# Half of an output sum moved from VectorE to accumulating transfers, and four more modulation products given to TensorE

## Chip, cores and metric

The kernel runs on one NeuronCore of one Trainium2 chip. The metric is device time in microseconds of one execution; the time before is the median of three runs. A separate execution was profiled, and its rows are those below.

## What is computed

Two layers of a diffusion backbone work on 512 latent tokens and 256 context tokens, each with 1024 features, in fp32. A layer is a SwiGLU feed-forward half (FFN), a mixing block, and a second FFN. Each FFN does

```python
y = swiglu(modulate(rms_norm(h, g), m[:, 3 * i], m[:, 3 * i + 1]), w1, w3, w2)
return h + 0.5 * m[:, 3 * i + 2, None, :] * y
```

where `m = silu(c) @ w + b` holds nine modulation vectors of 1024 for each layer, one set for the tokens and one for the context. The hidden width is 2816, in 22 blocks of 128.

## The kernel before

The residual `h` stands transposed in SBUF: eight tiles `h[d]` of 128 features by 768 columns, the context in columns 0 to 255 and the latent tokens in 256 to 767. Every fp32 product is made of three passes over split operands (`mm3`, lines 402 to 407): high times high, high times low, low times high. Weights are loaded raw by SP's queue and split by ScalarE (`L412`, or `L415` with a factor) and VectorE (`L413`, `L416`).

An FFN (`ffn7`) takes the 22 hidden blocks in 11 pairs. A middle pair (`pair`) computes its two blocks for both weight matrices with seven products in place of eight (Strassen's scheme), each of 24 matmuls 384 columns wide, in two PSUM tiles Y and X. The order in the program is: B11 into Y; then `middle()`, which is the whole w2 part of the pair before; then `y0`, a copy of Y that ScalarE makes (`snapshot`, line 742); B21 into X; E added into Y; t3 into X; t1, t4, B22. E may not begin before `y0` is taken, because it adds into the bank that `y0` copies; t3 may not begin before `gated` has read X and `y0`. Further copies (`y1` after E, `w0` after t3) follow in the same way.

`middle(j)` goes over the two halves of the eight tiles of `h`, in each half over the context columns and then the latent columns, in each over four tiles d: `down` makes 6 matmuls into one of four PSUM banks and VectorE adds the gated result into `h[d]` (line 760). When both halves are done, the pair's `g` tiles are given back, and `modulate(j)` puts `mods[j]` groups of modulation rows in the queue, at a much lower priority (`later(3000)`): each group loads four `ada` tiles (`mod_group`, line 500; on SP in the first FFN, on GpSimd's queue in the second) and VectorE makes six row-by-column products from them (line 492). In layer 0 the first FFN has such groups with middles 1 to 8 (`mods=(0,) + (2,) * 8`), the second with middles 2 to 7.

The order in which an engine takes its instructions is made when the kernel is built: the program order gives priorities, and a scheduler with a model of the engines places the ready instruction of highest priority. On the chip each engine then follows its own list.

SBUF tiles of 768 columns come from 44 slots. `m3` takes the slot that has been free for longest, `free` puts one at the end of the list:

```python
i = self.free_slots.popleft()
t = self.mp.tile([128, n], dt, tag=f"m{i}", name=self.name(base), bufs=1)
self.slot_of[t.tensor.name] = i
```

A new tile may be written only when every reader of the tile that had the slot before is done, transfers included. In a middle pair 35 slots are held: 16 by the normed input n, 12 by combinations of it, 3 by the broadcast condition, 4 by the g of the pair before. That leaves nine.

The start (`Start`, layer 0 only) makes the first 2048 modulation values. For each of eight feature tiles k, `item(k)` loads 1 MB of modulation weights, and `mods(k)` makes shift and scale: for k in `ON_PE` on TensorE (32 passes of 128x2, line 224, and two small VectorE instructions, line 228), for the others with VectorE (line 492) for the tokens and with GpSimd and ScalarE (lines 484 and 486) for the context. Then `norm(k)` makes the normed tile (lines 285 to 289), and 12 matmuls of 512 and 9 or more of 256 columns use it. Before, `ON_PE` is `(0,)`.

Of the kernel before, what the change touches and what calls it, by code (L numbers as in the profile page):

```python
# [11 lines left out]
AF = mybir.ActivationFunctionType  # L12
ALU = mybir.AluOpType
# [23 lines left out]
C_COLS = (0, CTX)  # L37
X_COLS = (CTX, T)
# [132 lines left out]
def mod_order(i):  # L171

    return (i // 2 + 8 * (i % 2)) if i < 16 else i


class Start:

    LAG = 1
    ON_PE = (0,)
    AHEAD = 2  # L180
    LOADS = 3

# [33 lines left out]
    def mods(self, k):  # L216

        b, nc = self.b, self.b.nc
        it = self.items.pop(k)
        if k in self.ON_PE:  # L220
            ps = b.ps("B", 3)
# [8 lines left out]
        else:  # L230
            for s in range(2):
                with b.later(60 * s):
                    for q in (1, 0):
                        b.mod_tile(0, q * 8 + k, s, (it[q], it[2][:, q * 256:q * 256 + 256]), pool=s == 1)
                    self.derive(k, s, 1)
        if k in self.ON_PE:
            self.derive(k, 0, 2)
# [84 lines left out]
class Builder:  # L322
# [335 lines left out]
        self.split_psum(w[:, 0], w[:, 1], r, scale)  # L658
        return w

    def ffn7(self, l, i, n, t, gate, nxt, streams=(X_COLS, C_COLS), split=None, late=None, mods=(), begin=None):

# [8 lines left out]
        nc = self.nc  # L673
# [75 lines left out]
            self.last_silu = nc.scalar.activation(s[:, cols], zv[:, 0], AF.Silu, scale=sign)  # L749
            nc.vector.scalar_tensor_tensor(out=s[:, cols], in0=zv[:, 1], scalar=sign, in1=s[:, cols], op0=ALU.mult, op1=ALU.mult)  # L750

        def down(fs, ws, d, cols):
            c0, c1 = cols
            s = 1 if c0 < CTX else 0
            ps = self.psB()
            for x in (1, 0):
                o = x * 512 + d % 4 * 128
                self.mm3(ps[:, 0:c1 - c0], [ws(d // 4)[:, p, o:o + 128] for p in range(2)],
                         (g[fs[x]][0][:, c0:c1], g[fs[x]][1][:, c0:c1]), x == 1, x == 0)
            nc.vector.scalar_tensor_tensor(out=self.h[d][:, c0:c1], in0=ps[:, 0:c1 - c0], scalar=gate()[:, d, s:s + 1],  # L760
                                           in1=self.h[d][:, c0:c1], op0=ALU.mult, op1=ALU.add)

# [86 lines left out]
        def second(j):  # L849

            ws = {}
            return lambda half: ws[half] if half in ws else ws.setdefault(half, self.unit(w2[j, half]))
# [53 lines left out]
        def middle(j):  # L906
            def go():
                ws, fs = second(j), (2 * j, 2 * j + 1)
                for half in range(2):
                    for cols in streams[::-1]:  # L910
                        for d in range(half * 4, half * 4 + 4):
                            down(fs, ws, d, cols)
                self.free([g.pop(f) for f in fs])
                modulate(j)
            return go

        def modulate(j):
            with self.later(3000):
                for _ in range(min(mods[j] if j < len(mods) else 0, len(self.mod_queue))):
                    self.mod_queue.pop(0)()  # L920
# [5 lines left out]
        fs = (NF - 2, NF - 1)  # L926
        if x_only:
            pair(np_ - 1, middle(np_ - 2))
        else:
            held = {}  # L930

            def go():
                held["ws"], held["fs"] = second(np_ - 2), (NF - 4, NF - 3)
                for d in range(8):
                    down(held["fs"], held["ws"], d, X_COLS)

            pair(np_ - 1, go)
            for d in range(8):
                down(held["fs"], held["ws"], d, C_COLS)
            self.free([g.pop(f) for f in held["fs"]])  # L940
            modulate(np_ - 2)
        ws = second(np_ - 1)
# [707 lines left out]
    def gate(self, l, mod, ns, f):  # L1650
        box = []

        def get():
            if not box:
                box.append(self.derive_gate(l, mod, ns, f))
            return box[0]
        return get

    def build(self, stop=None):
        nc = self.nc  # L1660
        self.setup()
        n = self.new_n()
        begin = Start(self, n)
        for g in range(5, 24):
            self.mod_queue.append(lambda g=g: self.mod_group(0, g, 16))
        for l in range(DEPTH):
            last = l == DEPTH - 1
            ns = 1 if last else 2
            nxt = Next(self, l, 3, SM_GMIX, 2, n)
            if l:  # L1670
                tabs = []
                self.ffn7(l, 0, n, t, self.gate(l, 2, 2, 0.5), nxt, late=lambda: tabs.extend(self.late_tables(l)), mods=(0,) * 2 + (2,) * 6)
            else:
                tabs = []
                self.ffn7(l, 0, n, {}, self.gate(l, 2, 2, 0.5), nxt, late=lambda: tabs.extend(self.late_tables(l)),
                          mods=(0,) + (2,) * 8, begin=begin)
            assert not self.mod_queue
            if l == 0:
                self.setup_mixing()
            if stop == (l, 0):  # L1680
                break

            nxt = Next(self, l, 6, SM_GF2, ns, keep=X_HALVES if last else T_HALVES)
            self.mixing(l, n, tabs, self.gate(l, 5, ns, 1.0), last, nxt)
            n, before = nxt.n, nxt
            if stop == (l, 1):
                break

            if not last:
                self.load_small(l + 1)  # L1690
                self.silu_c(wide=True)
                for g in range(24):
                    self.mod_queue.append(lambda g=g: self.mod_group(1, g))
                nxt = Next(self, l + 1, 0, SM_GF1, 2, n, keep=T_HALVES)
                self.ffn7(l, 1, n, before.t, self.gate(l, 8, 2, 0.5), nxt, mods=(0,) * 2 + (2,) * 6)
                t = nxt.t
            else:
                self.ffn7(l, 1, n, before.t, self.gate(l, 8, 1, 0.5), Done(self), streams=(X_COLS,), split=X_HALVES)
            if stop == (l, 2):
                break  # L1700
        if stop is not None:
            for k in range(8):
                nc.sync.dma_start(self.a["out"][k], self.h[k])
# [40 lines left out]
def pack(inp):  # L1744
# [12 lines left out]
    tra = np.concatenate([tra[..., 0:768].reshape(8, 128, 1536), tra[..., 768:].reshape(8, 128, 512)], -1)  # L1757
    o["ada0"] = np.stack([(nat if k in Start.ON_PE else tra)[k] for k in range(8)])
    wa = a["w_ada"].transpose(0, 2, 1).reshape(L, 72, 128, D)[:, [mod_order(i) for i in range(72)]]
# [65 lines left out]
```

## Time and profile before

| what | value |
|---|---|
| median of 3 runs | 2718.38 us (2717.03 to 2721.74) |
| profiled execution | 2715.82 us, span of the core 2714.0 us |
| mean granted TensorE clock | 0.982 of full speed |
| busy: TensorE / VectorE / ScalarE / GpSimd | 96% / 78% / 43% / 14% |

The busy shares are averages over the span. TensorE is granted one of two clock levels, 1.2 and 2.4 GHz, and a share of 1.00 means the higher one throughout. "Idle before" is the time that an engine did nothing ahead of an instruction, with the instruction or transfer that ended it.

### The profile page before, as it was taken

The numbers are of one execution on the slowest core, as the hardware profiler recorded it, in microseconds if no ns is written. First come the engines' busy times: TensorE is split into PE (matmuls) and PEld (weight loads), VectorE is DVE, ScalarE is ACT, GpSimd is POOL, SyncE is SP. The second block draws the span as 40 slices with busy tenths as digits, with TensorE's granted clock in tenths as the row PEclk, the third lists the DMA queues.
The fourth block names the chain that finished last, engine by engine and source line by source line (L and its number), as shares of the span: only waits on it lengthen the run. The fifth ranks groups of instructions, "written<-read, shape, count | busy, mean of one in ns | idle before, by whom it ended". The sixth has DMA issues, their size and how long they took to land.

```text
span 2714.0 us, 40079 instructions
## 1 busy us (share of the span) xinstructions
PE 2599.7 (96%) x15572; PEld 2351.3 (87%) x15572; DVE 2121.0 (78%) x3664; ACT 1168.5 (43%) x2042; POOL 383.8 (14%) x530
## 2 busy tenths in 40 slices
PE   6899999999989999999999999999999899999999
PEld 4788989898867778999899889999998777889998
DVE  8998989975685647899996778888766775588887
ACT  6532333244665654233333633323234765554443
POOL 4300000010352212010000211100001452110000
PEclk8999999999999999999999999999999999999999
DMA  6634444321200014344332334443221200143322
GB/s 242 164 115 123 131 122 135 117 84 53 74 24 17 20 47 101 120 137 133 119 99 71 80 92 140 137 149 121 82 86 53 80 15 24 42 114 108 95 94 93
DMA packets 81889, 261.51 MB, mean 96 GB/s; under 512 B 10018, under 2 KB 19874, under 8 KB 81700
## 3 DMA queue, kind: packets, MB, share of 16 engines
q1 hardware_dynamic: 64804, 209.67, 24.0%
q0 software_dynamic: 16896, 49.29, 7.4%
q8 instruction: 122, 2.00, 0.3%
q14 instruction: 67, 0.55, 0.1%
HBM read 245.29 MB, written 2.10 MB: 91 GB/s over the span
## 4 chain that ended last, share of the span: by engine, by line
PE 80%; DVE 10%; issue 3%; ACT 3%; DMA 3%; POOL 1%; SPq 0%; DVEq 0%; POOLq 0%; ACTq 0%
PE S L405 14%; PE S L407 14%; PE S L406 14%; PE B L405 10%; PE B L406 10%; PE B L407 10%; PE B L1334 3%; DVE cst L492 2%; PE B L1485 2%; DVE w L413 1%; DVE h L760 1%; DMA nf<-nf 1%; DMA ada<-in_w_ada 1%; PE B L1453 1%; DVE nf L285 1%
## 5 line engine op out<-in xcount | busy, mean ns | idle before, releaser
L412 ACT CAST w<-raw 128x1024 fp32r<-128x1024 f32 (+1 forms) x387 | 403.8, 1045 | 630.6 <-PE B L407 304.1
L413 DVE TENSOR_TENSOR w<-raw,w 128x1024 fp32r<-128x1024 f32 (+1 forms) x387 | 474.9, 1228 | 95.4 <-ACT w L412 94.3
L405 PE MATMUL S<-nhi,w 128*128 128x384 f32 (+2 forms) x1520 | 493.6, 331 | 38.0 <-ACT y L742 22.5
L406 PE MATMUL S<-nlo,w 128*128 128x384 f32 (+2 forms) x1520 | 499.9, 330 | 3.1 <-DVE nlo L615 2.0
L407 PE MATMUL S<-nhi,w 128*128 128x384 f32 (+2 forms) x1520 | 499.7, 330 | 1.0 <-DVE w L413 0.9
L760 DVE SCALAR_TENSOR_TENSOR h<-B,g,h 128x512 f32<-128x512 f32 (+1 forms) x616 | 377.3, 633 | 126.4 <-PE B L407 123.3
L406 PE MATMUL B<-glo,w 128*128 128x512 f32 (+1 forms) x1232 | 421.4, 346 | 0.0
L407 PE MATMUL B<-ghi,w 128*128 128x512 f32 (+1 forms) x1232 | 420.6, 345 | 0.0
L405 PE MATMUL B<-ghi,w 128*128 128x512 f32 (+1 forms) x1232 | 408.1, 347 | 7.6 <-DVE h L760 6.5
L405 PEld LDWEIGHTS S<-nhi,w 128*128 128x128 f32 x1520 | 288.9, 192 | 49.9 <-ACT y L742 24.9
L406 PEld LDWEIGHTS S<-nlo,w 128*128 128x128 f32 x1520 | 291.9, 192 | 11.7 <-DVE nlo L615 3.9
L406 PE MATMUL S<-clo,w 128*128 128x384 f32 (+1 forms) x936 | 301.4, 322 | 0.0
L405 PE MATMUL S<-chi,w 128*128 128x384 f32 (+1 forms) x936 | 301.3, 322 | 0.0
L407 PEld LDWEIGHTS S<-nhi,w 128*128 128x128 f32 x1520 | 291.4, 192 | 10.3 <-DVE w L413 4.4
L407 PE MATMUL S<-chi,w 128*128 128x384 f32 (+1 forms) x936 | 299.3, 323 | 0.0
L407 PEld LDWEIGHTS B<-ghi,w 128*128 128x128 f32 x1232 | 232.4, 189 | 30.1
L405 PEld LDWEIGHTS B<-ghi,w 128*128 128x128 f32 x1232 | 227.8, 188 | 35.4 <-DVE h L760 8.7
L406 PEld LDWEIGHTS B<-glo,w 128*128 128x128 f32 x1232 | 232.2, 188 | 25.3 <-issue 0.7
L492 DVE CUSTOM_DVE_ANT_0 cst<-ada,bc,mpart 128x768 f32<-128x768 f32 x238 | 246.3, 1035 | 3.2 <-DMA ada<-in_w_ada 1.6
L405 PEld LDWEIGHTS S<-chi,w 128*128 128x128 f32 x936 | 176.1, 188 | 3.7
L406 PEld LDWEIGHTS S<-clo,w 128*128 128x128 f32 x936 | 176.0, 188 | 3.2
L407 PEld LDWEIGHTS S<-chi,w 128*128 128x128 f32 x936 | 175.1, 188 | 2.2
(261 smaller groups left out, 4344.9 us busy)
## 6 DMA issues: line engine op xcount, KB each, us to landing
raw<-in_w13s SPq DMA_DIRECT2D x176, 512.0 KB, 3.4
raw<-in_w2s SPq DMA_DIRECT2D x88, 512.0 KB, 3.5
ada<-in_w_ada POOLq DMA_DIRECT2D x96, 384.0 KB, 3.8
ada<-in_w_ada SPq DMA_DIRECT2D x75, 384.0 KB, 3.7
nf<-nf POOLq DMA_DIRECT2D x48, 192.0 KB, 4.0
raw<-in_w_out SPq DMA_DIRECT2D x16, 512.0 KB, 3.8
ada<-in_ada SPq DMA_DIRECT2D x16, 384.0 KB, 5.9
raw<-in_w_in_t SPq DMA_DIRECT2D x10, 512.0 KB, 3.4
```

Of the source, the lines that this page charges most:

```text
L285: nc.vector.scalar_tensor_tensor(out=t, in0=b.h[k][:, c0:c1], scalar=a, in1=self.R[cols], op0=ALU.mult, op1=ALU.mult)
L405: mm(out, lhs[0], rhs[0], start=start, stop=False, skip_group_check=more)
L406: mm(out, lhs[0], rhs[1], start=False, stop=False, skip_group_check=more)
L407: mm(out, lhs[1], rhs[0], start=False, stop=stop, skip_group_check=more)
L412: nc.scalar.copy(hi, src)
L413: nc.vector.tensor_sub(lo, src, hi.bitcast(F32))
L492: nc.vector.tensor_tensor_reduce(out=self.junk[:, 0:w.shape[1]], in0=w, in1=v, scale=1.0, scalar=init, op0=ALU.mult, op1=ALU.add, accum_ou ...
L760: nc.vector.scalar_tensor_tensor(out=self.h[d][:, c0:c1], in0=ps[:, 0:c1 - c0], scalar=gate()[:, d, s:s + 1], in1=self.h[d][:, c0:c1], op0 ...
L1334: mm(outs[y], lhs[y], rhs[y], start=start, stop=stop)
L1453: nc.tensor.transpose(ps[0:96, t * 128 - c0:t * 128 - c0 + 128], src[half][t // 2][:, c:c + 96], self.ident)
L1485: nc.tensor.transpose(pt[:, x * 256 + i * 128:x * 256 + i * 128 + 128], Ps[i, y][:, tok(kp * 2 + x)], self.ident)
```

## The change

Two edits. First, `Start.ON_PE` becomes `(0, 1, 2, 4, 6)`: four more first tiles get their modulation from TensorE, and three stay with VectorE, GpSimd and ScalarE. Second, in layer 0's two FFNs, in the middles that have modulation groups, tiles d = 1, 3, 5 and 7 are no longer summed by VectorE: ScalarE copies the gated PSUM result into a tile `hsum`, and when a half's context and latent columns are both copied, GpSimd's queue issues one transfer for the whole tile that adds it into `h[d]`. A half takes two slots for its `hsum` tiles and gives them back behind the transfers.

```diff
-    ON_PE = (0,)
+    ON_PE = (0, 1, 2, 4, 6)
...
+            if aside is not None:
+                nc.scalar.activation(aside[:, c0:c1], ps[:, 0:c1 - c0], AF.Copy, scale=gate()[:, d, s:s + 1])
+                return
             nc.vector.scalar_tensor_tensor(out=self.h[d][:, c0:c1], in0=ps[:, 0:c1 - c0], scalar=gate()[:, d, s:s + 1],
                                            in1=self.h[d][:, c0:c1], op0=ALU.mult, op1=ALU.add)
...
                 for half in range(2):
+                    sums = {}
+                    if aside and mods[j:j + 1] > (0,):
+                        sums = {d: self.m3(base="hsum") for d in range(half * 4 + 1, half * 4 + 4, 2)}
                     for cols in streams[::-1]:
                         for d in range(half * 4, half * 4 + 4):
-                            down(fs, ws, d, cols)
+                            down(fs, ws, d, cols, sums.get(d))
+                    for d, t_ in sums.items():
+                        nc.gpsimd.dma_start(out=self.h[d], in_=t_, accum_op=ALU.add)
+                        self.free(t_)
...
-                          mods=(0,) + (2,) * 8, begin=begin)
+                          mods=(0,) + (2,) * 8, begin=begin, aside=True)
...
-                self.ffn7(l, 1, n, before.t, self.gate(l, 8, 2, 0.5), nxt, mods=(0,) * 2 + (2,) * 6)
+                self.ffn7(l, 1, n, before.t, self.gate(l, 8, 2, 0.5), nxt, mods=(0,) * 2 + (2,) * 6, aside=True)
```

## Rows read from the trace of the kernel before

**Rows 1.** The page, part 1: busy time, share of the span, instructions.

```profile
PE 2599.7 (96%) x15572; PEld 2351.3 (87%) x15572; DVE 2121.0 (78%) x3664; ACT 1168.5 (43%) x2042; POOL 383.8 (14%) x530
```

**Rows 2.** Windows: length, busy time (instructions) per engine, clock, DMA share, GB/s.

```profile
24.00:100.00 76.00, 52.86 (x223) 41.71 (x224) 75.10 (x146) 44.15 (x107) 43.73 (x35) 0.82 0.63 194
163.19:558.54 395.35, 377.65 (x2105) 358.90 (x2104) 369.63 (x701) 120.98 (x153) 0.00 (x0) 0.97 0.39 122
1137.81:1421.98 284.17, 279.31 (x1587) 266.33 (x1586) 269.82 (x503) 90.20 (x113) 21.58 (x40) 0.99 0.40 124
```

**Rows 3.** TensorE's waits in the last two of these stretches: total, times, longest.

```profile
PE S L405 <- ACT y L742: 17.7, 4, 6.3
...
PE S L405 <- ACT y L742: 4.8, 1, 4.8
```

**Rows 4.** Timeline of TensorE around two such waits: start, duration, line, shapes.

```profile
233.28 0.39 PE L406 MATMUL B<-glo,w 128*128 128x512 f32 x1
...
234.21 0.39 PE L407 MATMUL B<-ghi,w 128*128 128x512 f32 x1
240.88 0.69 PE L405 MATMUL S<-nhi,w 128*128 128x384 f32 x1 [6.28 <-ACT y L742]
...
245.50 0.34 PE L407 MATMUL S<-nhi,w 128*128 128x384 f32 x1
...
337.08 0.44 PE L405 MATMUL S<-nhi,w 128*128 128x384 f32 x1 [1.83 <-ACT y L742]
...
337.77 0.52 PE L405 MATMUL S<-nhi,w 128*128 128x384 f32 x1
```

**Rows 5.** Timeline of ScalarE: a copy of 512 PSUM columns, and two copies y.

```profile
26.76 0.59 ACT L274 COPY R<-B 128x512 f32<-128x512 f32 x1 [4.27 <-PE B L570]
...
206.07 0.80 ACT L742 COPY y<-S 128x768 f32<-128x768 f32 x1 [2.39 <-DVE glo L724]
...
240.03 0.80 ACT L742 COPY y<-S 128x768 f32<-128x768 f32 x1 [4.35 <-DVE mT L492]
```

**Rows 6.** VectorE, 163.19 to 558.54: line 760 by shape; line 492 in all.

```profile
L760 DVE SCALAR_TENSOR_TENSOR h<-B,g,h 128x512 f32<-128x512 f32 x65 | 47.9, 747 | 5.5 <-PE B L407 5.4
L760 DVE SCALAR_TENSOR_TENSOR h<-B,g,h 128x256 f32<-128x256 f32 x64 | 29.6, 479 | 2.1 <-PE B L407 1.8
...
163.19:558.54 395.35, 142.28 (x379) 0.97 0.39 122
```

**Rows 7.** Timeline of TensorE, start of a pair: B11, context sums, B21, latent sums.

```profile
255.63 0.34 PE L405 MATMUL S<-nhi,w 128*128 128x384 f32 x1
...
259.62 0.34 PE L407 MATMUL S<-nhi,w 128*128 128x384 f32 x1
...
260.26 0.28 PE L406 MATMUL B<-glo,w 128*128 128x256 f32 x1
...
262.51 0.28 PE L407 MATMUL B<-ghi,w 128*128 128x256 f32 x1
262.63 0.33 PE L405 MATMUL S<-nhi,w 128*128 128x384 f32 x1
...
266.80 0.39 PE L405 MATMUL B<-ghi,w 128*128 128x512 f32 x1
```

**Rows 8.** GpSimd's accumulating transfers of 192 KB, line 694: issue; landing; their queue, 1010 to 1042.

```profile
L694 POOL DMA_DIRECT2D nf<-nf x64: 853/874/1545, 65.0 to 2392.6; - x64
...
DMA to landing us min/median/max: 3.0/3.6/5.7
...
q0 software_dynamic: 2159, 2.95, 57.0%
```

**Rows 9.** The start: line 224; line 492 from 24 to 100; one VectorE instruction beside GpSimd's.

```profile
L224 PE MATMUL B<-ccol,ada x32: 353/353/373, 9.5 to 16.1; 128*128 128x2 f32 x32
...
24.00:100.00 76.00, 34.05 (x64) 0.82 0.63 194
...
69.32 5.61 DVE L287 SCALAR_TENSOR_TENSOR nlo<-nf,mT,nhi 128x256 fp32r<-128x256 f32 x1
```

More of the change, by code (lines that the diff above doesn't have):

```diff
@@ L659, in split_block, with ffn7 @@
         return w
-    def ffn7(self, l, i, n, t, gate, nxt, streams=(X_COLS, C_COLS), split=None, late=None, mods=(), begin=None):
+    def ffn7(self, l, i, n, t, gate, nxt, streams=(X_COLS, C_COLS), split=None, late=None, mods=(), begin=None, aside=False):
         nc = self.nc
@@ L750, in gated, with down @@
             nc.vector.scalar_tensor_tensor(out=s[:, cols], in0=zv[:, 1], scalar=sign, in1=s[:, cols], op0=ALU.mult, op1=ALU.mult)
-        def down(fs, ws, d, cols):
+        def down(fs, ws, d, cols, aside=None):
             c0, c1 = cols
```

## Prediction

> **What bounds the kernel now.** I began with the page's busy line: TensorE is busy for 96% of the span [rows 1], so a change can win only where TensorE waits or runs at its lower clock. Then I cut the span into windows. Three stretches matter here [rows 2]. In the start (24 to 100 us) VectorE is busy 75.1 of 76 us and TensorE 52.9 at a clock share of 0.82: VectorE is the bound. From 163 to 559 us lie eight pairs of layer 0's first FFN, each window edge being the same instruction of a pair (ScalarE's split for E, line 415). VectorE is busy 93% of it, TensorE 96% at a clock of 0.97; a pair takes 395.35 / 8 = 49.4 us. From 1138 to 1422 lie the six pairs of the second FFN that the change touches: 284.17 / 6 = 47.4 us, and TensorE hardly rests.
>
> How short can a pair be? I took steps from start to start at the full clock. A product's matmul takes (259.62 - 255.63) / 23 = 0.1735 us, a context matmul of a sum (262.51 - 260.26) / 19 = 0.118 [rows 7], a latent one (234.21 - 233.28) / 4 = 0.2325 [rows 4]. A pair has 168, 48 and 48 of them: 29.2 + 5.7 + 11.1 = 46.0 us. So the eight pairs lose 27.4 us in all, the six pairs 8.2 us. That is the most that relief of VectorE can return there.
>
> Third view, TensorE's waits: 17.7 and 4.8 us, all for the copy y [rows 3]. The timeline of ScalarE says why that copy is late: it waits for VectorE's modulation products (mT, line 492) or for VectorE's last read of an older tile (glo, line 724) [rows 5]. Neither makes data for y; both are readers of the tile that had y's slot before. Slots are what binds, and the change takes four more per pair.
>
> **Who gets which slot.** Nine slots are free at a middle, first in, first out. Before: the two modulation groups take eight, the four g slots come back behind the nine, and y0 takes the ninth, which the last silu tile of the pair before gave back; that is the glo wait of [rows 5], so the count holds. After: hsum 1, 3, 5, 7 take the first four and go back behind the other five; then come the four g; the eight ada tiles take the five and hsum 1, 3 and 5. The next free slot is that of hsum 7, and y0 takes it. So y0 now waits for the last accumulating transfer of the same middle, which waits for the last sum matmul of that middle, and E waits for y0. Before, E ran between the sums. In exchange y1 and w0, whose waits made most of the loss before, get ada slots that are loaded from tiles free since the pair before, so those waits should go.
>
> **Edit by edit, per pair.**
> VectorE gives up eight sums: 4 x 0.747 + 4 x 0.479 = 4.9 us [rows 6]. It stops being the bound; at most the 27.4 and 8.2 us above come back.
> ScalarE gets eight copies. The 512-column copy took 0.59 [rows 5]; with 256 columns at no more than that, 2.4 to 4.7 us. It was busy 31% of the stretch [rows 2], so seven of the eight are hidden beside sum matmuls; the last is on the path.
> GpSimd issues four transfers at 0.87 us each [rows 8]; idle otherwise, only the last counts, inside its landing time.
> Transfer queues: 15 transfers of 192 KB (2.95 MB) took 57% of 16 engines over 32 us, 1.2 us each [rows 8], so one of 384 KB about 2.4, four 9.7 us of a pair at a share of 0.39 [rows 2]: room enough.
> The ada loads of the second group now stand in SP's (second FFN: GpSimd's) queue behind hsum's transfers, and the next raw weights behind them; weights have been loaded up to a pair ahead, so I price this at nothing. If that cover is gone, it is the third rival.
>
> The new wait, step by step from the last sum matmul: ScalarE copy 0.59; landing of a 384 KB accumulate; y0 0.80; some 0.15 for three hand-overs (estimate). The landing isn't in the trace. Bounds: below, the 192 KB median 3.6; above, the longest of those, 5.7 [rows 8]. I take 3.6 + 1.2 for the second half of the bytes = 4.8. Sum 6.3 us. What could TensorE do meanwhile? E, t1 and t4 need y0, t3 needs X read together with y0. Only B21 is left, and the list before runs it between context and latent sums (B21 begins at 262.63, latent sums at 266.80) [rows 7], as filler until g is ready. So I take the wait as bare. The Trainium skill ("DMA: Bandwidth & Descriptors", section "Anatomy of one DMA — SWDGE (gpsimd) path") fits 2.0 us plus bytes at 436 GB/s; that would be 2.9 us for the landing, a wait of 4.4 and a time some 27 us below mine. The rows show 3.6 where that rule gives 2.5, so the rows decide.
>
> The clock: after a wait of 6.28 us the next 14 matmuls took 245.50 - 240.88 = 4.62 us, not 14 x 0.1735 = 2.43, so 2.2 us were lost at the lower level. It fell even after a wait of 1.83 us (0.52 a matmul from 337.77) [rows 4]. Cost: 6.3 + 2.2 = 8.5 us, a pair of 54.5.
>
> Behind y0 in ScalarE's list stand the weight splits for E and t3; they too come late, but TensorE waits for y0 anyway.
>
> First FFN: 8 x 54.5 - 395.4 = +40.6. Second: 6 x 54.5 - 284.2 = +42.8.
>
> **The start.** Eight modulation pieces leave VectorE (two for each of four tiles): 34.05 us over 16 such pieces [rows 9] is 2.1 each, so 17 us. They were stretched by GpSimd (an instruction of 256 columns took 5.61 [rows 9]), and GpSimd loses four sevenths of that work. TensorE gets 32 passes per tile: 7.0 us at the lower clock (9.5 to 16.5), half at the higher; four tiles 14 to 28. TensorE's sum in the 76 us becomes 67 to 81, less up to 9.5 if the clock of 0.82 rises (52.86 x 0.18). So VectorE no longer bounds the start, TensorE does: -18 to +5 us. I take -6.
>
> Sum: 2715.8 (the profiled execution) + 40.6 + 42.8 - 6 = 2793. The median of the runs is 2.6 above that execution, so I give 2794, between the two. Its own range, from landing and start: 2768 to 2818.
>
> **Rivals.**
> *B21 behind the sums.* If the new list runs latent sums before B21, 4.2 us (24 x 0.1735) of the wait are filled: 14 x 4.2 = 58 us less, 2736; half of it 2765. For it: VectorE is freer, so g may be ready sooner. Against: g's last parts go through ScalarE, which gets busier. 15%.
> *Faster.* The wait isn't bare or doesn't exist, and all pairs run at 46.0: -27.4 - 8.2 - 6, 2674. It decides where a pair loses under 3.0 us, clock included ((395.4 + 284.2 + 6) / 14 - 46.0): a landing under 1.5 us, or B21 behind the sums and no fall of the clock. For it: VectorE at 93% is a true bound in the first FFN. Against: 3.0 is the shortest landing in view [rows 8]. 13%.
> *More waits.* hsum's slots come from the second modulation group of the pair before. VectorE spends 142.28 / 8 = 17.8 us a pair on these products [rows 6], at the lowest priority; if two of twelve are late, 3 us more with PSUM banks held: 14 x 3 = 42, 2836. Against: a pair of 54.5 leaves VectorE 13 us free. The Trainium skill ("SBUF — State Buffer", section "SBUF: two separate sides") warns that VectorE can lock GpSimd out of writing descriptors, which would lengthen the landing; no row here shows it, the issue of 0.87 being steady beside a busy VectorE. 12%.
> *Gain and loss cancel*, with the wait about three quarters hidden: 5%, 2718.
>
> The main case keeps 55%. A change under 0.2% (5.4 us) is about what a measurement here can't tell from none. Faster 13%, same 5%, slower 82%. The range 2715 to 2845 leaves out the faster case and a tail above.
>
> **What would show it.** Right: TensorE waits some 14 times, 5 to 8 us, ahead of E for the copy y, and y waits for a transfer; E no longer mixed with sums; the lower clock after each; y1's waits gone; a pair near 54.5 in both FFNs; the start some 6 us shorter. Wrong: y0 taken before the transfers land, or B21 seen between the last sum and E, or pairs near 46.

## The result and the profile after

The changed kernel takes 2805.2 us (median of 4 runs, 2799.3 to 2808.4) against 2719.2 for the one before beside it: 1.031 times as long, 95% interval 1.029 to 1.033. That is slower, 11 us above the forecast of 2794. The profiled execution took 2808.4 us with a span of 2806.6, 92.6 us more than the span before.

The page's busy line, which answers [rows 1]:

```profile
PE 2637.8 (94%) x15700; PEld 2393.1 (85%) x15700; DVE 2047.4 (73%) x3512; ACT 1220.7 (43%) x2122; POOL 409.3 (15%) x570
```

VectorE has 74 us less to do, TensorE 38 us more, and its share of the span fell. The windows, with the edges of [rows 2] (ScalarE's split for E, line 415, of the same pairs; columns as there):

```profile
24.00:100.00 76.00, 73.65 (x393) 65.29 (x394) 64.33 (x140) 39.05 (x82) 31.87 (x28) 0.96 0.83 245
148.38:590.00 441.62, 382.35 (x2088) 363.70 (x2087) 342.73 (x632) 158.19 (x218) 27.79 (x32) 0.93 0.52 142
1175.41:1514.86 339.45, 288.74 (x1563) 274.36 (x1563) 256.85 (x470) 118.19 (x162) 44.86 (x67) 0.92 0.49 135
```

In the start TensorE is now busy nearly throughout, and its clock share rose from 0.82 to 0.96. In the eight pairs VectorE fell from 93% to 78%, as intended, and still they take 441.62 / 8 = 55.2 us each and not 49.4; the six pairs 56.6 and not 47.4. The view of waits shows what TensorE does instead (total, times, longest; the first line is of the whole span, the next two of the eight pairs, the last two of the six):

```profile
PE S L405 <- ACT y L743: 110.0, 14, 9.9
...
PE S L405 <- ACT y L743: 59.3, 8, 8.1
...
ACT y L743 <- DMA h<-hsum: 43.8, 8, 6.2
...
PE S L405 <- ACT y L743: 50.7, 6, 9.9
...
POOL ada L500 <- DMA h<-hsum: 76.8, 16, 7.8
```

Fourteen waits, one for each pair with transfers, all for the copy y; in the eight pairs y in turn waits eight times for an accumulating transfer, and in the six pairs six times. The waits of [rows 3] were 17.7 and 4.8. In the six pairs GpSimd's loads wait for these transfers as well, sixteen times. The timeline of one pair's end of sums, all engines (start, duration, engine, line):

```profile
329.52 0.69 ACT L762 ACTIVATE hsum<-B,g 128x512 f32<-128x512 f32 x1 [0.70 <-PE B L407]
...
330.61 0.87 POOL L921 DMA_DIRECT2D h<-hsum  x1 [0.51 <-ACT hsum L762]
...
331.83 0.39 PE L407 MATMUL B<-ghi,w 128*128 128x512 f32 x1
...
337.79 0.80 ACT L743 COPY y<-S 128x768 f32<-128x768 f32 x1 [4.49 <-DMA h<-hsum]
...
338.64 0.69 PE L405 MATMUL S<-chi,w 128*128 128x384 f32 x1 [6.42 <-ACT y L743]
339.12 0.52 PE L406 MATMUL S<-clo,w 128*128 128x384 f32 x1
...
343.92 0.38 PE L406 MATMUL S<-clo,w 128*128 128x384 f32 x1
```

The last transfer is issued at 330.61, while the last sum is still running: the scheduler placed the tiles that go by transfer ahead of VectorE's two. y0 can start only 7.18 us later, and TensorE rests from 331.83 + 0.39 to 338.64. Then 16 matmuls, from 338.64 to 343.92, take 5.28 us where 16 x 0.1735 = 2.78 would do [rows 7].

Where the 92.6 us of span came from, by the starts of E:

| stretch | before | after | difference |
|---|---|---|---|
| start, to the first of these E | 163.19 | 148.38 | -14.8 |
| eight pairs, first FFN | 395.35 | 441.62 | +46.3 |
| from there to the six pairs | 579.27 | 585.41 | +6.1 |
| six pairs, second FFN | 284.17 | 339.45 | +55.3 |
| the rest | 1292.02 | 1291.74 | -0.3 |

Of the +6.1, 5.1 lie directly behind the eight pairs (162.60 us where 157.46 stood). There TensorE waits no longer than before; the stretch holds 1000 of its instructions in place of 987 and runs at a clock of 0.98 in place of 1.00. The eight pairs hold 2088 in place of 2105. So part of it is work that stands behind the edge now, and belongs to the eight pairs.

### The profile page after: what moved, and what is told of

Read it like the earlier page. It is cut to its first block, busy times and chain, and to the rows that moved or that the text cites. A ratio compares the mean times of both kernels' runs of the same rounds, so it can differ in the third digit from the quotient of the medians.

```text
span 2806.6 us, 40409 instructions
## 1 busy us (share of the span) xinstructions
PE 2637.8 (94%) x15700; PEld 2393.1 (85%) x15700; DVE 2047.4 (73%) x3512; ACT 1220.7 (43%) x2122; POOL 409.3 (15%) x570
## 4 chain that ended last, share of the span: by engine, by line
PE 47%; DMA 3%; issue 3%; DVE 2%; ACT 2%; POOL 1%; POOLq 0%; ACTq 0%; DVEq 0%
PE S L405 9%; PE S L407 9%; PE S L406 9%; PE B L405 6%; PE B L406 6%; PE B L407 6%; DMA h<-hsum 2%; PE B L1344 1%; PE B L1495 1%; DMA nf<-nf 1%; POOL h L921 0%; PE B L1463 0%; DMA raw<-in_w13s 0%; ACT w L412 0%; DVE nm L1327 0%
## 5 line engine op out<-in xcount | busy, mean ns | idle before, releaser
L405 PE MATMUL S<-chi,w 128*128 128x384 f32 (+1 forms) x936 | 316.8, 339 | 110.0 <-ACT y L743 110.0
L764 DVE SCALAR_TENSOR_TENSOR h<-B,g,h 128x256 f32<-128x256 f32 (+1 forms) x504 | 313.0, 637 | 127.8 <-PE B L407 124.8
L406 PE MATMUL S<-clo,w 128*128 128x384 f32 (+1 forms) x936 | 314.2, 336 | 0.0
L407 PE MATMUL S<-chi,w 128*128 128x384 f32 (+1 forms) x936 | 311.5, 335 | 0.0
L405 PEld LDWEIGHTS S<-chi,w 128*128 128x128 f32 x936 | 186.4, 199 | 118.3 <-ACT y L743 116.0
L492 DVE CUSTOM_DVE_ANT_0 cst<-ada,bc,mpart 128x768 f32<-128x768 f32 x230 | 234.0, 1017 | 57.3 <-DMA ada<-in_w_ada 54.3
L743 ACT COPY y<-S 128x768 f32<-128x768 f32 (+1 forms) x117 | 87.2, 746 | 282.9 <-PE S L407 199.9
L406 PEld LDWEIGHTS S<-clo,w 128*128 128x128 f32 x936 | 186.2, 199 | 2.3
```

Source lines behind the costliest of these rows:

```text
L405: mm(out, lhs[0], rhs[0], start=start, stop=False, skip_group_check=more)
L406: mm(out, lhs[0], rhs[1], start=False, stop=False, skip_group_check=more)
L407: mm(out, lhs[1], rhs[0], start=False, stop=stop, skip_group_check=more)
L492: nc.vector.tensor_tensor_reduce(out=self.junk[:, 0:w.shape[1]], in0=w, in1=v, scale=1.0, scalar=init, op0=ALU.mult, op1=ALU.add, accum_ou ...
L743: nc.scalar.copy(v, both(bank))
```

## The experiments

All were timed in turn with the kernel before on the same chip; ratios are to that. The stretches are those of the table above, each from one profiled execution.

| run | time, us | ratio (95%) | first E | 8 pairs | 6 pairs |
|---|---|---|---|---|---|
| y0's tile taken early | 2689.1 | 0.987 to 0.990 | 150.0 | 378.7 | 292.9 |
| slots given back in another order | 2710.1 | 0.996 to 0.999 | 149.2 | 388.7 | 294.6 |
| even tiles | 2791.3 | 1.025 to 1.028 | 148.6 | 438.9 | 324.0 |
| TensorE's modulation alone | 2699.9 | 0.991 to 0.995 | 148.4 | 393.0 | 282.1 |
| transfers alone | 2822.8 | 1.039 to 1.042 | 164.9 | 440.9 | 336.8 |
| three transfers | 2786.6 | 1.025 to 1.029 | 148.4 | 426.8 | 334.4 |
| transfers by stream | 2797.5 | 1.028 to 1.031 | 147.8 | 438.1 | 329.7 |
| loads on SyncE's queue | 2800.8 | 1.029 to 1.032 | 149.7 | 441.3 | 332.2 |
| early, loads on SyncE's queue | 2679.0 | 0.986 to 0.988 | 147.7 | 376.9 | 286.5 |
| early, transfers in the first FFN only | 2679.5 | 0.985 to 0.989 | 149.3 | 376.1 | 284.7 |
| early in both, transfers in the first only | 2678.1 | 0.985 to 0.988 | 148.6 | 377.8 | 280.6 |
| early in both, no transfers | 2681.5 | 0.986 to 0.989 | 146.7 | 377.5 | 282.2 |

**Is it the slot?** Two runs change which slot y0 gets and nothing that is computed. The first takes y0's tile from the pool ahead of the sums:

```diff
-        def snapshot(bank, base):
-            y = self.m3(2 * wd, base=base)
+        def snapshot(bank, base, y=None):
+            y = self.m3(2 * wd, base=base) if y is None else y
...
+            y = self.m3(2 * wd, base="y") if aside and not begin_pair(j) and mods[j - 1:j] > (0,) else None
             middle()
...
-            y0 = snapshot(Y, "y")
+            y0 = snapshot(Y, "y", y)
```

> The changed kernel, but y0's tile is taken ahead of the sums of the pair, so that it gets the oldest free slot and not the one that the last accumulating transfer gives back. All work stays. Slot theory: the 14 waits of 7.9 us ahead of E (110 us in all, and some 2 us each at the lower clock behind them) go, E runs between the sums again: 2660 to 2700 us. Rival (the transfers or ScalarE's copies are too slow as such, or the transfers hold up h for the next pair): TensorE's waits stay near 110 us, at other copies, and the time at 2780 to 2810.

The second keeps every allocation where it was and only gives the four slots back in another order, so that y0 gets the one whose transfer was issued a half earlier:

```diff
+                back = []
                 for half in range(2):
...
-                        self.free(t_)
+                    back.insert(0, list(sums.values()))
+                self.free(back)
```

> The changed kernel, with the four hsum slots of a pair given back in another order: half 1's (tiles 5, 7) ahead of half 0's (1, 3), all at the end of the sums. y0 then gets the slot of tile 3's sum, whose transfer was issued half a middle earlier (some 8 us). No instruction of the program is added, moved or left out; only addresses change. Slot theory: the 14 waits go: 2660 to 2700 us. Rival (total load of the transfers, or of ScalarE): 2790 to 2810.

Measured: 2689.1 and 2710.1 us, where the changed kernel takes 2805.2. The same transfers, copies and matmuls are in all three. In the first, the longest group of TensorE's waits for y or for what makes it is this (waits of TensorE, whole span):

```profile
PE S L405 <- DVE y L749: 9.8, 5, 3.7
```

In the second, waits of TensorE in the whole span, and of ScalarE in the eight pairs:

```profile
PE S L405 <- ACT y L743: 6.4, 7, 2.0
...
ACT y L743 <- DMA h<-hsum: 24.0, 8, 3.8
```

There y0 still waits for a transfer, as its new slot has it, but for one of the first half, 5.4 to 7.4 us after its issue, and the second half's sums are left to TensorE meanwhile. 110.0 us of waits became 6.4. So the slot makes the fourteen waits; the rival, a load that is too high as such, has fallen. The second came out 10 us above its range: I had taken that transfer as landed long before, and it isn't.

**Do the two parts add up?** The second part alone, and the first alone:

```diff
-                          mods=(0,) + (2,) * 8, begin=begin, aside=True)
+                          mods=(0,) + (2,) * 8, begin=begin)
...
-                self.ffn7(l, 1, n, before.t, self.gate(l, 8, 2, 0.5), nxt, mods=(0,) * 2 + (2,) * 6, aside=True)
+                self.ffn7(l, 1, n, before.t, self.gate(l, 8, 2, 0.5), nxt, mods=(0,) * 2 + (2,) * 6)
```

> The kernel before with the second part of the change alone: TensorE modulates five first tiles, no sum goes by a transfer. Theory: only the start gets shorter, by the 14.8 us that stand between the two kernels at the first E: 2700 to 2707 us. Rival (the 14.8 us come from the first pair's sums, which the transfers take, or are lost again later because pairs bound by VectorE begin sooner and still end together): 2712 to 2720.

```diff
-    ON_PE = (0, 1, 2, 4, 6)
+    ON_PE = (0,)
```

> The changed kernel with one first tile on TensorE, as before, and the transfers left in. Theory: the two parts add up, so this loses what TensorE's modulation of five tiles gives by itself (14.8 to 18.4 us): 2818 to 2826 us. Rival (the transfers' waits swallow the start's gain, or part of the gain came from the sums that the transfers take from VectorE in the first pairs): 2803 to 2814.

Measured: 2699.9, which is 18.4 us below the kernel before beside it, and 2822.8, which is 17.6 above the changed kernel by the medians and 24 by the two ratios (1.040 and 1.031); the first E comes 16.6 us later. Within what is measured they add up: the modulation gives some 18 us, the transfers cost some 104 (1.031 less 0.993, times 2718). How the start gets shorter shows in the windows up to the first E, of the kernel before and of the changed one:

```profile
0.00:163.19 163.19, 128.92 (x614) 106.00 (x615) 142.13 (x267) 82.69 (x170) 54.99 (x50) 0.92 0.61 186
```

```profile
0.00:148.38 148.38, 143.00 (x746) 125.26 (x747) 115.94 (x237) 73.03 (x137) 32.31 (x34) 0.98 0.63 196
```

TensorE gets 132 instructions more, 128 of them the passes, and 14.1 us of busy time; its idle time falls from 34.3 to 5.4 us, 28.9 less. The passes by themselves (line 224 in the same two windows, TensorE's busy time first):

```profile
0.00:163.19 163.19, 6.99 (x32) 6.90 (x32) 0.92 0.61 186
...
0.00:148.38 148.38, 28.89 (x160) 29.28 (x160) 0.98 0.63 196
```

The four tiles' passes cost 21.9 us: those of two tiles start 0.21 us apart, as the first tile's do, those of the other two 0.11. TensorE's other work took 7.8 us less, with the clock share up from 0.92 to 0.98.

**What sizes the wait?** Three edits of the changed kernel, with y0's late slot kept. Even tiles in place of odd ones:

```diff
-                        sums = {d: self.m3(base="hsum") for d in range(half * 4 + 1, half * 4 + 4, 2)}
+                        sums = {d: self.m3(base="hsum") for d in range(half * 4, half * 4 + 4, 2)}
```

> The changed kernel with the even tiles of h (0, 2, 4, 6) by transfer in place of the odd ones: the last of the four transfers then follows the third sum of a half and not the fourth, and is issued one latent sum (some 1.4 us) earlier; y0 takes the slot of tile 6's sum. Slot theory: each of the 14 waits is some 1.4 us shorter: 2780 to 2792 us. Rival (the wait is set by something other than the last transfer): 2800 to 2810.

Three tiles in place of four:

```diff
-                        sums = {d: self.m3(base="hsum") for d in range(half * 4 + 1, half * 4 + 4, 2)}
+                        sums = {d: self.m3(base="hsum") for d in ((1, 3), (7,))[half]}
```

> The changed kernel with three tiles by transfer in place of four: tile 5's sums go back to VectorE, so that tile 7's transfer is the only one of its half; y0 still gets tile 7's slot. In the first FFN y0 starts some 8.0 us after the issue of tile 7's transfer. Theory 1 (it lands late because tile 5's transfer, issued 1.4 us ahead of it, is still being moved): it lands 1.5 to 2.5 us sooner, 14 waits shorter by as much: 2770 to 2785 us. Theory 2 (a transfer of this size takes that long by itself): 2800 to 2808.

Each transfer cut in two:

```diff
                             down(fs, ws, d, cols, sums.get(d))
-                    for d, t_ in sums.items():
-                        nc.gpsimd.dma_start(out=self.h[d], in_=t_, accum_op=ALU.add)
+                            if d in sums:
+                                nc.gpsimd.dma_start(out=self.h[d][:, slice(*cols)], in_=sums[d][:, slice(*cols)], accum_op=ALU.add)
+                    for t_ in sums.values():
                         self.free(t_)
```

> The changed kernel with each tile's transfer cut in two, context columns (128 KB) issued right behind their sum and latent columns (256 KB) behind theirs; y0 keeps its late slot. Theory (landing goes with the bytes that are still to be moved: a lone one of 384 KB let y0 start 6.1 us after its issue, one behind another of its size 8.1): 256 KB behind 256 KB gives some 6 us, 1 to 2 us less per wait: 2775 to 2790 us. Rival (each transfer costs its own time whatever its size, and twice as many crowd GpSimd's queue): 2800 to 2825.

The even tiles gave 2791.3, in the theory's range, but mostly not for its reason: the eight waits sum to 55.4 us in place of 59.3, 0.5 us each and not 1.4, since the scheduler had the transferred tiles first in either case. The six of the second FFN sum to 39.2 in place of 50.7, and that is the queue of the next question: in this run all six last transfers go out right behind their copies. Three tiles gave 2786.6, 1.6 us above the range. In the eight pairs y0 starts 6.1 us (mean) after the issue of the last transfer in place of 8.2, and the waits sum to 45.5, 1.7 us less each, as theory 1 has it; in the second FFN they fell by 0.8 only (46.1). Landing, of all transfers of the run with three (minimum, median, maximum), and the queue's rows of the run by stream (KB, median to landing):

```profile
DMA to landing us min/median/max: 3.9/5.5/7.5
```

```profile
h<-hsum POOLq DMA_DIRECT2D x56, 256.0 KB, 5.3
...
h<-hsum POOLq DMA_DIRECT2D x56, 128.0 KB, 4.4
```

By stream it was 2797.5, in neither range. A third of the bytes still takes 4.4 us and two thirds 5.3, where the whole takes 6.0. The waits sum to 101.0 us in place of 110.0, but the gain lies in the second FFN (43.3 in place of 50.7); in the first, whose loads are not in GpSimd's queue, it is 0.2 us a wait (57.7 in place of 59.3).

What else a landing is made of shows in the view of the DMA queues (packets, MB, share of the 16 engines' time; q0 is GpSimd's queue, q1 SyncE's), in the changed kernel from the last issue at 330.61 to y0 at 337.79:

```profile
q0 software_dynamic: 288, 0.79, 57.0%
q1 hardware_dynamic: 245, 0.79, 39.3%
```

The 16 engines are busy 96% of this time. In it they move both transfers of the half, 57.0% of 7.18 us or 2.05 us each, and weight loads of SyncE's queue for another 2.8. So most of this landing is the time in which the engines work off what has been issued to them. Without tile 5's transfer 2.05 us should go, and 2.1 went. The loads are the other part; no run took them away by themselves.

**Why is the second FFN's wait longer?** There the modulation weights come through GpSimd's queue. The timeline of GpSimd in the changed kernel, second FFN:

```profile
1243.45 0.55 POOL L500 DMA_DIRECT2D ada<-in_w_ada  x1 [4.26 <-DMA h<-hsum]
1244.10 0.87 POOL L921 DMA_DIRECT2D h<-hsum  x1
1251.46 0.55 POOL L500 DMA_DIRECT2D ada<-in_w_ada  x1 [6.50 <-DMA h<-hsum]
1252.12 1.82 POOL L921 DMA_DIRECT2D h<-hsum  x2
```

The copy y0 of that pair, by ScalarE's timeline, and the DMA queues from 1253.05, where the last of the two is issued, to y0:

```profile
1258.96 0.80 ACT L743 COPY y<-S 128x768 f32<-128x768 f32 x1 [6.66 <-DMA h<-hsum]
```

```profile
q0 software_dynamic: 372, 1.20, 93.9%
```

A load that gets the slot of an earlier sum waits 6.50 us for its transfer to land, and the pair's last two transfers, whose copies began at 1247.14 and 1248.53, stand behind it until 1252.12. Held back, the last one then lands sooner: y0 starts 5.9 to 6.3 us after its issue in the six pairs, 7.2 to 8.8 in the eight, and in the pair shown SyncE's queue moves nothing beside it. Loads through SyncE's queue, in the changed kernel and in the one with the early tile:

```diff
-            (self.nc.gpsimd if l else self.nc.sync).dma_start(t, self.a["w_ada"][l, g][:, i * 768:i * 768 + 768])
+            self.nc.sync.dma_start(t, self.a["w_ada"][l, g][:, i * 768:i * 768 + 768])
```

> The changed kernel with one edit: the second FFN's modulation weights are loaded through SyncE's queue, so that in GpSimd's queue no load that waits for a slot stands ahead of an accumulating transfer. y0 keeps its late slot. In the changed kernel TensorE's waits for y were 7.4 us each in the first FFN, whose loads go through SyncE, and 8.5 us in the second, and a pair took 55.2 and 56.6 us. Theory (GpSimd's queue makes the difference): the six waits fall to some 7 us and the six pairs to 54 to 55.2 us each: 2792 to 2798 us. Rival (the loads then hold the weights of the next pair in SyncE's queue): 2803 to 2815.

> The first experiment (y0's tile taken ahead of the sums), and the second FFN's modulation weights are loaded through SyncE's queue and not GpSimd's, so that no load that waits for a slot stands ahead of an accumulating transfer. Theory (that queue costs the second FFN's six pairs the difference between 48.8 and 47.3 us each): 2678 to 2683 us. Rival (the loads then hold up the w1, w3 and w2 weights behind them in SyncE's queue): 2690 to 2705.

In the first, GpSimd's timeline and TensorE's waits in the six pairs:

```profile
1244.17 0.86 POOL L921 DMA_DIRECT2D h<-hsum  x1 [4.58 <-ACT hsum L762]
1245.56 0.88 POOL L921 DMA_DIRECT2D h<-hsum  x1 [0.53 <-ACT hsum L762]
```

```profile
PE S L405 <- ACT y L743: 44.0, 6, 7.9
```

The last two transfers go out behind their copies, y0 starts 7.7 to 8.7 us after the issue, the six waits are 7.3 us each in place of 8.5, the six pairs 332.2 us in place of 339.5; the eight pairs, untouched, are the same within 0.3. The medians differ by 4.4 us and their intervals overlap, so the stretch shows it and the whole time hardly does (it lies between the two ranges). With the early tile the six pairs fell by 6.5 us, and the time to 2679.0, as the theory has it, though its interval of the ratio just overlaps that of the first experiment.

**What are the transfers worth, once the slot is right?**

```diff
-                self.ffn7(l, 1, n, before.t, self.gate(l, 8, 2, 0.5), nxt, mods=(0,) * 2 + (2,) * 6, aside=True)
+                self.ffn7(l, 1, n, before.t, self.gate(l, 8, 2, 0.5), nxt, mods=(0,) * 2 + (2,) * 6)
```

> y0's tile taken ahead of the sums, as in the first experiment, and transfers in the first FFN alone; the second FFN adds all of w2's sums with VectorE, as before. In the first experiment six pairs of the second FFN took 292.9 us, without transfers 282.1. Theory: that difference comes back, 2676 to 2681 us. Rival (those pairs only catch up what stays late elsewhere): 2686 to 2692.

The next two take y0's tile early in both FFNs, the one with transfers in the first FFN, the other with none (`aside=True` gone there too):

```diff
-            y = self.m3(2 * wd, base="y") if aside and not begin_pair(j) and mods[j - 1:j] > (0,) else None
+            y = self.m3(2 * wd, base="y") if not begin_pair(j) and mods[j - 1:j] > (0,) else None
```

> Transfers in the first FFN alone, and y0's tile taken ahead of the sums in both FFNs. In the second FFN only one wait of 4.8 us for y is left to remove: 2672 to 2677 us. Rival (slots are not what made that wait): 2679 to 2682.

> The same as the run beside it, with no transfers at all: every sum is added by VectorE, TensorE modulates five first tiles, y0's tile is taken ahead of the sums. It tells whether the gain of the earlier runs is the transfers' or the slot's. If VectorE is the bound of the first FFN's pairs (93% busy before), they stay near 49 us and it is 2693 to 2700 us. If the slot alone made the loss, the pairs go to 47.3 and it is 2674 to 2682.

2679.5, then 2678.1, just above its range and not to be told from the one before it (its six pairs are 4 us shorter), and 2681.5. The last decides what bounds the eight pairs: near 49 us each was expected if VectorE does. The windows of the eight pairs, with transfers and without:

```profile
148.56:526.32 377.76, 372.46 (x2118) 352.87 (x2117) 338.50 (x637) 155.22 (x218) 27.79 (x32) 1.00 0.61 166
```

```profile
146.69:524.14 377.45, 373.74 (x2121) 356.14 (x2120) 364.65 (x683) 121.05 (x154) 0.00 (x0) 0.99 0.41 128
```

Without transfers VectorE is busy 97% of the stretch, more than before, and the pairs take the same 47.2 us. Relief of VectorE by 26 us gives back nothing: the stretch with transfers is 0.3 us longer, less than one profiled execution can tell.

## Why the prediction was right, and what it mis-sized

Its mechanism was right in each step that decides. y0 takes the slot of the last sum, waits for that transfer, and E waits for y0: fourteen times, bare, with matmuls at the lower clock behind each; the waits for y1 are gone. Two runs that change the slot alone take the waits away. Its rival on the faster side put the break-even at 3.0 us lost per pair and the time at 2674 if nothing is lost; the run that gets nearest, at 47.2 a pair, has 2678.

The sum missed by 15.2 us of span (77.4 forecast, 92.6 measured), in these terms:

- The new wait, forecast at 6.3 us, was 59.3 / 8 = 7.4 and 50.7 / 6 = 8.5. In the first FFN two errors offset each other, which is luck. The landing was too low by some 3.3 us: 4.8 in the sum, with 5.7 as the bound above, where y0 starts 7.2 to 8.8 us after the issue (8.2 in the mean). The step behind it is "room enough", read from a share of 0.39 that is an average over the pairs. Where the landing lies, the engines are 96% busy, with the transfer issued 1.4 us earlier (without it y0 starts 2.1 us sooner) and with SyncE's loads. Against that, ScalarE's copy was not on the path, since the transferred tiles are summed ahead of VectorE's: the last transfer is issued 1.6 us before the last sum ends (330.61 to 332.22), and not 0.59 behind it.
- The queue of GpSimd was priced at nothing, and costs 7.3 us in the second FFN. That is what is left of a larger cost: the last transfers go out some 3 us later, and land some 2 us sooner, than with the loads on SyncE's queue. I had looked at loads behind transfers, and only at what they delay; the reverse, a transfer behind a load that waits for an earlier transfer, was the cost.
- The clock, forecast at 2.2 us a pair, was 2.5 in the pair shown; by the steps of the matmuls behind each of the fourteen waits it was 1.6 to 2.9, 2.2 in the mean. A pair is then 46.0 + 7.4 + 1.8 = 55.2 and 46.0 + 8.5 + 2.1 = 56.6, where 1.8 and 2.1 are what remains for the clock and all else; 54.5 was forecast. So +46.3 for +40.6, and +55.3 for +42.8.
- The start gave 14.8 us and not 6. The four tiles' passes cost 21.9 us, in the middle of the 14 to 28, TensorE's other work there took 7.8 us less, so that its busy time grew by 14.1, and its idle time, which I had cut by too little, almost vanished. This is the error on the other side.
- Between the stretches, 6.1 us that I had at nothing; in part it is work moved across the edge.

One reading was wrong without moving the sum. I took VectorE, 93% busy, as a bound of the eight pairs whose relief could give back up to 27.4 us, and kept 13% for that. The run without transfers gets 15.6 us back by y0's slot alone (393.0 with TensorE's modulation, 377.5 with the early tile too), with VectorE 97% busy; TensorE's waits for y fall from 20.5 to 6.1 us. The range "2768 to 2818" comes out of the bounds named for it as 2765 to 2818, on which nothing rests.

The third rival, hsum's copies late for want of slots, did not come: TensorE's waits name none of it in the changed kernel. The Trainium skill ("SBUF — State Buffer", section "SBUF: two separate sides") has GpSimd unable to write descriptors while VectorE runs an instruction in a two-port mode; the issue stayed at a median of 0.870 us over 56 transfers, 1.175 at most, so this kernel doesn't show it. The rule in the Trainium skill ("DMA: Bandwidth & Descriptors", section "Anatomy of one DMA — SWDGE (gpsimd) path") gives an estimate of 2.9 us for 384 KB; the runs measured a median of 6.0, and 5.5 with three transfers a pair, on engines that moved other transfers too, so the rows were the better guide, and even they were too low.

## What to carry to other kernels

Where tiles come from a common pool in turn, count who gets the slot that a slow reader gives back: an edit that borrows a few tiles can put a transfer's landing in front of a copy that never touches that data, and one allocation moved up is the cure. Whether there is room for a transfer is read from the DMA engines in the microseconds in which it has to land (96% busy here), and not from an average (39%). A high busy share beside a wait is no bound until the wait is taken away; here 93% looked like the limit and 97% was no hindrance. And if an edit in two parts comes out slow, run the parts alone: 18 us of gain was hidden under 104 of loss, and the version that keeps it, with the early tile and no transfers at all, has 0.987 times the time of the kernel before.

## What the runs showed of the hardware

All transfers of the changed kernel (GpSimd, line 921: duration of the issue; landing):

```profile
L921 POOL DMA_DIRECT2D h<-hsum x56: 860/870/1175, 154.6 to 1479.8; - x56
...
DMA to landing us min/median/max: 4.0/6.0/8.8
```

An accumulating transfer from tile to tile lands in 4.4, 5.3 and 6.0 us for 128, 256 and 384 KB (medians of two runs), while the plain loads of 384 KB in the same queue take 3.6. These are landings beside other transfers, and size alone does not set them: the accumulating transfers of 192 KB (line 694 before) land in 3.8 us in the changed kernel. Of the 16 engines one of 384 KB takes (0.52 x 441.62 - 0.39 x 395.35) / 32 = 2.4 us by the shares in the windows, as the prediction had from the 192 KB row [rows 8], or 2.05 us by the packets between 330.61 and 337.79. The rest of the landing there is mostly the other transfers on the same engines, which are 96% busy.

After a wait of 6.42 us TensorE starts its matmuls 0.32 us apart, and 0.17 apart again only from 343.92 on, 5.28 us after the start. The clock share of the eight pairs is 0.97 before, 0.93 with their eight waits, and 0.99 to 1.00 in the runs with y0's tile taken early.
